# Two matmuls in place of three for each weight block: both parts of the activations side by side under the high weights, and the halves of a PSUM bank added behind

## The chip, the core and the metric

One core of one Trainium2 chip runs the whole program. The metric is the device time of the program in microseconds (us). TensorE (PE) multiplies, VectorE (DVE), ScalarE (ACT) and GpSimd (POOL) do everything elementwise, and SyncE (SP) issues the transfers of the weights. In the views, PEld is the weight load of a matmul, which overlaps the matmuls.

## The reference, cut to what matters

A trunk of two decoder layers over 256 tokens with 1024 channels, all in float32. Layer 0 mixes tokens with a short gated convolution, layer 1 with dilated windowed attention (8 heads in each of 3 groups, 128 channels a head, rotary on 32 of them). After each mixer comes a squared-ReLU MLP of 4096 channels and a gated per-layer input; a last rmsnorm ends it.

```python
def rmsnorm(x, g): return x * lax.rsqrt(jnp.mean(x * x, axis=-1, keepdims=True) + RMS_EPS) * g

def short_conv_mixer(h, w_in, w_conv, w_out):
    gate_b, gate_c, xin = jnp.split(h @ w_in, 3, axis=-1)
    y = gate_b * causal_depthwise_conv(gate_c * xin, w_conv)
    return y @ w_out

def squared_relu_mlp(h, w_up, w_down):
    return jnp.square(jax.nn.relu(h @ w_up)) @ w_down
```

The attention's three groups are weighed by the softmax of their log-sums of exponentials, so that one softmax over all keys of the three groups gives the same. The per-layer input is `sigmoid(rmsnorm(x) @ w_gate) * (p @ w_proj)`, added to x.

## The kernel before

**Products.** Every operand of a large product is held as two float32r parts, high and low, so that value = high + low, and a product is the sum of three: high weights by high activations, high weights by low activations, low weights by high activations. Activations lie with channels on partitions and the 256 tokens along a row. A *block* is one 128x128 piece of weights; in most stages ("w" blocks, channels by tokens) the weights are the stationary side, and `block()` issues three matmuls of 256 columns each (L804) that add into one half of an accumulator. An accumulator is one bank of PSUM, 128 partitions by 2 halves of 256, for two neighbouring blocks of columns ("a pair of columns"). There are 1808 such blocks. In the "t" blocks (the attention's v, the last gate and projection) the activations are stationary, and the three matmuls have 384 or 512 columns of weights.

**Weights.** They come in slabs of up to 8 blocks (512 KB) by one transfer each (L767), 273 in all, into RAW_BUFS buffers. `split_to` splits each slab: ACT copies it to the high part `whi` (L777), DVE subtracts to get the low part `wlo` (L269, in the helper `sub`, which every low part goes through). `weights` asks for the slab that stands LOOK = 5 ahead of the one in use, so that the splits stand among the other work of ACT and DVE in the order of the plan.

**Order.** `make_plan` writes PE's work as a list; the steps in it ("do") add what the other engines do. The Tile scheduler orders each engine's instructions by their place in the plan, with the steps named in URGENT and the small chain of a norm moved ahead by HURRY = 250 places. Each engine then works through its own list in order, and waits where an operand isn't there.

**Stages.** In order of time: the projection of layer 0 (`acc_p`), the conv's products C, X, B for four pairs of columns, each followed by `conv`; the mixer's output (`acc_o`, `mix_out`); up (`acc_u`, 16 pairs, `up_out` behind each); down (`acc_d`), all four pairs side by side for 24 of the 32 rows of blocks, then pair by pair; the gate (`acc_g`, `gate_out`), with the projection multiplied in; then heads 0 to 7: q and k of three groups (`acc_qk`, `qk_out`: times cosr L1037, two rotary pieces L1040, added on POOL L1046), v (`v_out`), and among the next head's products the scores, the turn (transposes `tp`, L1090) and the values (`o`); then w_o, up, down and the last gate with the final norm.

**Norms.** `h_ready` (L836, L837) makes the two parts `xh`, `xl` of h times the gain, and `squares` (L847, L849, L851) adds up the squares of a token on POOL. The 1/rms joins later: `stat` (ssq, L872 to L905) makes it a diagonal, `spread` (L913, L915) turns that into a row on every partition, and the row is multiplied in behind the product (L980, L991, L1011, L1022). In the conv stage `spread` stands in the middle of the first B.

Of the kernel before, what the change touches and what calls it, by code (L numbers as in the profile page):

```python
# [34 lines left out]
RAW_BUFS, SPLIT_BUFS, ACT_BUFS = 6, 7, 45  # L35

# Rows of a head: the rotary halves lie 32 partitions apart.
# [27 lines left out]
def mlp_plan(layer):  # L65
# [11 lines left out]
    nf = FF // P  # L77
# [32 lines left out]
def last_plan():  # L110
    """The second layer's gate, projection and the final norm, by tokens."""
# [27 lines left out]
def make_plan():  # L139
    plan = [("do", "begin")]  # L140
    plan += proj_plan()
    for c in range(NP):
        for s, what in ((1, "C"), (2, "X"), (0, "B")):
            for k in range(NK):
                for i in (0, 1):
                    plan.append(("w", "sc_in", k, s * NK + 2 * c + i, (what, c), i, "x0"))
                if (c, s, k) == (0, 0, 4):
                    plan.append(("do", "spread", 0))
            if (c, s) == (0, 1):
                plan.append(("do", "stat", 0))  # L150
        plan.append(("do", "conv", c))
    for k in range(4):
        for j in range(NP):
            for i in (0, 1):
                plan.append(("w", "sc_out", k, 2 * j + i, ("o", j), i, "y"))
    for j in range(NP):
        for k in range(4, NK):
            for i in (0, 1):
                plan.append(("w", "sc_out", k, 2 * j + i, ("o", j), i, "y"))
        plan.append(("do", "mix_out", 0, j))  # L160
# [17 lines left out]
    plan += v(0, (0,)) + [("do", "spread", 3)]  # L178
    plan += [("do", "qk_out", 0, g) for g in range(GROUPS)] + v(0, range(1, NK)) + [("do", "v_out", 0)]
    for h in range(1, HEADS):  # L180
        plan += qk(h, 0, range(NK)) + [("do", "qk_out", h, 0)]
        plan += qk(h, 1, range(NK)) + [("do", "scores", h - 1)] + [("do", "qk_out", h, 1)]
        plan += qk(h, 2, range(NK)) + [("do", "turn", h - 1)] + [("do", "qk_out", h, 2)]
        plan += v(h, range(4)) + [("do", "values", h - 1)] + v(h, range(4, NK)) + [("do", "v_out", h)]

    def wo(j, ks):
        return [("w", "w_o", k, 2 * j + i, ("o", j), i, "y") for k in ks for i in (0, 1)]

    last = HEADS - 1
    plan += [x for k in (0, 1) for j in range(NP) for x in wo(j, (k,))]  # L190
    plan.append(("do", "scores", last))
    plan += [x for k in (2, 3) for j in range(NP) for x in wo(j, (k,))]
    plan.append(("do", "turn", last))
    plan += wo(0, (4, 5, 6)) + wo(1, (4,)) + [("do", "values", last)]
    for j in range(1, NP):
        plan += wo(j, (5, 6) if j == 1 else (4, 5, 6)) + wo(j - 1, (7,)) + [("do", "mix_out", 1, j - 1)]
    plan += wo(NP - 1, (7,)) + [("do", "mix_out", 1, NP - 1)]
# [8 lines left out]
def columns(key, col):  # L206
    """The columns of a weight matrix that one block of the plan takes, in order."""
# [10 lines left out]
def make_slabs(plan):  # L218
    """Runs of weight blocks that are loaded together: [[(key, k, col, width)]]."""
# [16 lines left out]
def tile_trunk(ctx: ExitStack, tc: tile.TileContext, plan, slabs, ap, out):  # L236
# [16 lines left out]

    def bank(name):
# [28 lines left out]
    for op in plan:  # L283
        if op[0] != "do":
            key = (op[4], op[5])
# [45 lines left out]
    def block(kind, key, k, col, name, half, operand, m=0, cuts=1):  # L331
        if name not in opened:
            acc[name] = bank("acc_" + "_".join(map(str, name)))
        left[name, half] -= 1
        whi, wlo = weights((key, k, col))
        x = [t[:, k % 2, :] for t in state[operand][k // 2]]
        if kind == "w":
            dst = acc[name][:, half, :]
            pairs = ((whi, x[0]), (whi, x[1]), (wlo, x[0]))
        else:  # L340
# [3 lines left out]
            xhi, xlo = (t[:, half * P : (half + 1) * P] for t in x)  # L344
            pairs = ((xhi, whi), (xhi, wlo), (xlo, whi))
        for n, (a, b) in enumerate(pairs):
            nc.tensor.matmul(
                dst,
# [3 lines left out]
                stop=n == 2 and left[name, half] == 0,  # L352
# [4 lines left out]
    def close(name):  # L357
        opened.discard(name)
        # Names are used again in the second layer.
        return acc.pop(name)  # L360

# [1 line left out]
    def split_into(kind, j, src, cuts=1):  # L363
        if kind in ("p0", "p1"):
            hi, lo = held("ph", f"{kind}h", 1, F32R), held("pl", f"{kind}l", 1, F32R)
        else:
            hi, lo = act(f"{kind}h{j}", F32R), act(f"{kind}l{j}", F32R)
# [4 lines left out]
        state[kind][j] = (hi, lo)  # L372

    def h_ready(n, j):
        """h[j] holds norm n's input."""
        hi, lo = act(f"xh{n}_{j}", F32R), act(f"xl{n}_{j}", F32R)
# [4 lines left out]
        state[f"x{n}"][j] = (hi, lo)  # L381
        squares(n, j)

    def squares(n, j):
        """The squares' sum over the channels that a partition holds."""
        sq = act(f"sq{n}_{j}")
        if j == NP - 1 and n in (2, 3, 5):
            nc.scalar.activation(sq, h[j], AF.Square)
        else:
            nc.gpsimd.tensor_tensor(sq, h[j], h[j], ALU.mult)  # L390
        tot = act(f"tot{n}_{j}")
        nc.gpsimd.tensor_tensor(tot[:, 0, :], sq[:, 0, :], sq[:, 1, :], ALU.add)
        if j:
            nc.gpsimd.tensor_tensor(tot[:, 1, :], tot[:, 0, :], cur["sq"], ALU.add)
# [7 lines left out]
    def newton(v, name):  # L402
        """v ** -0.5"""
# [7 lines left out]
    def stat(n):  # L411
        """1 / rms of a token, on the token's partition: column 2 b for half b."""
# [21 lines left out]
    def stat_rows(n):  # L434
        """1 / rms ** 2 of each token, on each partition."""
# [14 lines left out]
    def spread(n):  # L450
        """A column's values, on each partition."""
# [7 lines left out]
        if n == 3:  # L459
            # Rows without a rotary half have angle 0.  # L460
# [4 lines left out]
    def begin():  # L465
# [3 lines left out]
        # The array's clock is low until it has worked for a while: products of ones until the weights are here.  # L469
# [48 lines left out]
    def conv(c):  # L518
        pc, px, pb = close(("C", c)), close(("X", c)), close(("B", c))
        cx = spool.tile([P, 2, S + 2], F32, tag="cx", name=f"cx{c}")  # L520
        nc.gpsimd.memset(cx[:, :, 0:2], 0.0)
        t = act(f"ct{c}")
        nc.vector.tensor_tensor(t, pc, both(rows[0, 2]), ALU.mult)
        nc.vector.tensor_tensor(cx[:, :, 2:], t, px, ALU.mult)
# [8 lines left out]
        b = act(f"cb{c}")  # L533
        nc.vector.tensor_tensor(b, pb, both(rows[0]), ALU.mult)
        nc.vector.tensor_tensor(b, b, z, ALU.mult)
        split_into("y", c, b)

    def mix_out(layer, j):
        nc.vector.tensor_tensor(h[j], close(("o", j)), h[j], ALU.add)
        h_ready(3 * layer + 1, j)  # L540

    def up_out(j):
        p = close(("u", j))
        r = act(f"r{j}")
        nc.scalar.activation(r, p, AF.Relu)
        hi, lo = act(f"uh{j}", F32R), act(f"ul{j}", F32R)
# [745 lines left out]
```

## Time and profile before

| | |
|---|---|
| three timed runs | 813.25, 813.15, 810.01 us; median 813.15 us |
| the profiled execution: span from its first to its last instruction | 809.0 us |
| its own time around the span | not given; the runs above lie 1.0 to 4.2 us over the span |
| DVE, PE groups, ACT, POOL | 736, 6282, 538 and 110 records |
| HBM read | 139.10 MB, 173 GB/s over the span |

The span is the profiled execution's own time as far as the page gives it. Each group of instructions is named by line, engine and operation, with output and inputs by the program's names. "Idle before" is the time that an engine stood still just before an instruction, and the name behind the arrow is what ended it. The DMA engines are busy for 55.3% of the span with the weights:

```profile
q1 hardware_dynamic: 41616, 140.17, 55.3%
```

Stages of the trace: the first product at 4.47 us, C at 13.52, the mixer's output at 87.23, up at 110.27, down at 202.66, gate at 294.83, q and k of head 0 at 319.70, head 1 at 348.87, w_o at 558.96, the second up at 586.06, down at 679.19, the last gate at 771.35; the last product ends near 800.4.

### The profile page before, as it was taken

What the parts mean: (1) busy time and instruction counts of PE and PEld (TensorE: products, weight loads), DVE (VectorE), ACT (ScalarE), POOL (GpSimd) and SP (SyncE); (2) the same over time, 40 slices, a digit from 0 to 9 for tenths busy, and PEclk for the clock granted to TensorE, in tenths of its full rate; (3) what the DMA queues carried; (4) which work ended last, traced back from release to release, by engine and by line L of the source; (5) the groups of instructions that cost most, each with busy time, mean ns of one, the idle gap of its engine ahead of it and who ended that gap; (6) DMA issues with size and microseconds to landing.
All of it is one profiled execution on the core that took longest, in us unless ns stands there. A gap on an engine that the chain in (4) does not pass through costs nothing.

```text
span 809.0 us, 15204 instructions
## 1 busy us (share of the span) xinstructions
PE 789.9 (98%) x6282; PEld 782.5 (97%) x6282; DVE 578.5 (71%) x736; ACT 401.1 (50%) x538; POOL 131.7 (16%) x110
## 2 busy tenths in 40 slices
PE   7999999999999999899999999999999999999996
PEld 7999999999999999898999999999999999999985
DVE  7986697686444588898868877877697666444855
ACT  7544456565433455545445445545565555333543
POOL 6100060000000154331121111211240000000331
PEclk9999999999999999999999999999999999999999
DMA  8876646656666653645455555455455555565511
GB/s 274 282 240 200 183 150 199 201 162 203 182 183 184 183 173 116 196 163 162 155 164 161 154 174 159 137 187 182 146 178 187 183 183 182 183 182 182 170 40 52
DMA packets 41684, 141.13 MB, mean 174 GB/s; under 512 B 4752, under 2 KB 5136, under 8 KB 41616
## 3 DMA queue, kind: packets, MB, share of 16 engines
q1 hardware_dynamic: 41616, 140.17, 55.3%
q8 instruction: 49, 0.80, 0.4%
q14 instruction: 19, 0.16, 0.1%
HBM read 139.10 MB, written 1.05 MB: 173 GB/s over the span
## 4 chain that ended last, share of the span: by engine, by line
PE 55%; DVE 2%; POOL 0%; issue 0%; POOLq 0%; DVEq 0%; ACT 0%; ACTq 0%
PE acc_qk L804 14%; PE acc_d L804 11%; PE acc_u L804 11%; PE acc_v L804 8%; PE acc_o L804 3%; PE acc_g L804 3%; PE tp L1090 1%; PE o L1111 1%; PE sc L1072 1%; DVE wlo L269 1%; PE o L1105 1%; PE sc L1069 1%; PE acc_p L804 1%; DVE rot L1040 0%; PE rows L1141 0%
## 5 line engine op out<-in xcount | busy, mean ns | idle before, releaser
L269 DVE TENSOR_TENSOR wlo<-raw,whi 128x1024 fp32r<-128x1024 f32 (+3 forms) x273 | 341.1, 1257 | 167.7 <-ACT whi L777 166.6
L777 ACT ACTIVATE whi<-raw 128x1024 fp32r<-128x1024 f32 (+3 forms) x273 | 277.0, 1017 | 295.0 <-PE acc_d L804 103.2
L804 PE MATMUL acc_u<-xl,whi 128*128 128x256 f32 x512 | 145.2, 284 | 0.3 <-DVE xl L837 0.3
L804 PE MATMUL acc_d<-uh,wlo 128*128 128x256 f32 x512 | 145.0, 283 | 0.0
L804 PE MATMUL acc_d<-uh,whi 128*128 128x256 f32 x512 | 145.0, 283 | 0.0
L804 PE MATMUL acc_d<-ul,whi 128*128 128x256 f32 x512 | 145.0, 283 | 0.0
L804 PE MATMUL acc_u<-xh,whi 128*128 128x256 f32 x512 | 145.0, 283 | 0.0
L804 PE MATMUL acc_u<-xh,wlo 128*128 128x256 f32 x512 | 145.0, 283 | 0.0
L804 PE MATMUL acc_qk<-xh,whi 128*128 128x256 f32 x384 | 109.3, 285 | 0.0
L804 PE MATMUL acc_qk<-xh,wlo 128*128 128x256 f32 x384 | 108.6, 283 | 0.0
L804 PE MATMUL acc_qk<-xl,whi 128*128 128x256 f32 x384 | 108.6, 283 | 0.0
L804 PEld LDWEIGHTS acc_u<-xl,whi 128*128 128x128 f32 x512 | 97.0, 189 | 0.6 <-DVE xl L837 0.5
L804 PEld LDWEIGHTS acc_u<-xh,whi 128*128 128x128 f32 x512 | 97.0, 189 | 0.0
L804 PEld LDWEIGHTS acc_u<-xh,wlo 128*128 128x128 f32 x512 | 97.0, 189 | 0.0
L804 PEld LDWEIGHTS acc_d<-uh,wlo 128*128 128x128 f32 x512 | 96.6, 189 | 0.0
L804 PEld LDWEIGHTS acc_d<-ul,whi 128*128 128x128 f32 x512 | 96.6, 189 | 0.0
L804 PEld LDWEIGHTS acc_d<-uh,whi 128*128 128x128 f32 x512 | 96.6, 189 | 0.0
L804 PEld LDWEIGHTS acc_qk<-xl,whi 128*128 128x128 f32 x384 | 73.5, 191 | 0.0
L804 PEld LDWEIGHTS acc_qk<-xh,wlo 128*128 128x128 f32 x384 | 73.5, 191 | 0.0
L804 PEld LDWEIGHTS acc_qk<-xh,whi 128*128 128x128 f32 x384 | 73.5, 191 | 0.0
L1046 POOL TENSOR_TENSOR qk<-qk,rot 48x512 f32<-48x512 f32 x24 | 44.6, 1858 | 172.8 <-DVE rot L1040 172.8
L847 POOL TENSOR_TENSOR sq<-h 128x512 f32<-128x512 f32 x11 | 18.3, 1667 | 225.9 <-DVE h L1012 166.8
(196 smaller groups left out, 1427.8 us busy)
## 6 DMA issues: line engine op xcount, KB each, us to landing
raw<-in_w SPq DMA_DIRECT2D x232, 512.0 KB, 3.6
raw<-in_w SPq DMA_DIRECT2D x32, 384.0 KB, 3.1
raw<-in_w SPq DMA_DIRECT2D x7, 256.0 KB, 6.0
h<-in_xT SPq DMA_DIRECT2D x4, 256.0 KB, 6.5
out<-ht SPq DMA_DIRECT2D x4, 256.0 KB, 2.0
pt<-in_pT SPq DMA_DIRECT2D x2, 256.0 KB, 4.2
mask<-in_mask SPq DMA_DIRECT2D x2, 256.0 KB, 4.2
gain<-in_gain SPq DMA_DIRECT2D x2, 256.0 KB, 4.2
```

The lines of the kernel that those rows point to most:

```text
L269: nc.vector.tensor_tensor(out, a, f32(b), ALU.subtract)
L777: nc.scalar.activation(hi[:, :width], t[:, :width], AF.Copy)
L804: nc.tensor.matmul(dst, a, b, start=n == 0 and name not in opened, stop=n == 2 and left[name, half] == 0, skip_group_check=True,)
L847: nc.gpsimd.tensor_tensor(sq, h[j], h[j], ALU.mult)
L1046: nc.gpsimd.tensor_tensor(t[:48], t[:48], r[:48], ALU.add)
L1069: nc.tensor.matmul(ps[:, :S], q[:, 0, own], k[:, 1, :], start=n == 0, stop=n == 2)
L1072: nc.tensor.matmul(ps[:, (g + 1) * P : (g + 2) * P], t[:, 0, own], t[:, 1, own], start=True, stop=True)
L1090: nc.tensor.transpose(ps[n // 2][:, n % 2, b * P : (b + 1) * P], sm[:, n * P : (n + 1) * P], ident)
L1105: nc.tensor.matmul(ps[:, 0, :], a, b[:, kb, :], start=kb == 0 and n == 0, stop=False, skip_group_check=True)
L1111: nc.tensor.matmul(ps[:, 0, b * P : (b + 1) * P], v12[:, b, g * P : (g + 1) * P], t[:, g, b * P : (b + 1) * P], start=False, stop=g == 1, ...
```

## The change

**Pairs.** The two parts of an activation lie side by side in one tile (`pair`, 128 x 2 parts x 2 x 256). A "w" block is two matmuls: low weights by the high part (256 columns) into the first half of a bank, and high weights by both parts (512 columns) over the whole bank. So each block of columns has a bank of its own (`acc_u_8_0`, `acc_u_8_1` where one `acc_u_8` was), and its value is the sum of the two halves.

**Sums.** What reads an accumulator adds the halves first. `sums` does it by an ACT copy of the second half and a DVE add of the first, for each of the two blocks (up, down, projection, gate, q and k, C, X, B); `add_banks` does it by two DVE adds for each block (the mixers' outputs).

**Moves.** `qk_out`'s product with cosr goes from DVE to POOL, and the rotary pieces read SBUF where they read PSUM. The conv's two products with the rows of 1/rms go from DVE to POOL. The squares go from POOL to ACT (all of them) and their sums from POOL to DVE. `up_out` takes maximum and square in one DVE instruction, ACT makes a copy in place of ReLU and square.

**Plan.** Down goes pair by pair over all 32 rows of blocks (with two banks for a pair, four pairs side by side would fill all eight banks). The mixers' outputs go by two pairs. In head 0 the sums of q and k come ahead of two rows of v's blocks, and `spread` behind them.

**Buffers.** RAW_BUFS 6 to 5, SPLIT_BUFS 7 to 6, the general ones 45 to 13 and 20 pairs. The order of the transfers stays. The comments and a first, unused copy of the inner functions are deleted, so that the line numbers fall.

```diff
-RAW_BUFS, SPLIT_BUFS, ACT_BUFS = 6, 7, 45
+RAW_BUFS, SPLIT_BUFS, ACT_BUFS, PAIR_BUFS = 5, 6, 13, 20
...
-    for k in range(nf - 8):
-        for j in range(NP):
-            for i in (0, 1):
-                plan.append(("w", down, k, 2 * j + i, ("d", j), i, "u"))
     for j in range(NP):
-        for k in range(nf - 8, nf):
+        for k in range(FF // P):
...
+    plan += [("do", "add_up", ("qk", 0, g)) for g in range(GROUPS)]
+    plan += v(0, (0, 1)) + [("do", "spread", 3)]
+    plan += [("do", "qk_out", 0, g) for g in range(GROUPS)] + v(0, range(2, NK)) + [("do", "v_out", 0)]
...
         if kind == "w":
-            dst = acc[name][:, half, :]
-            pairs = ((whi, x[0]), (whi, x[1]), (wlo, x[0]))
+            dst = acc[name]
+            products = ((dst[:, 0, :], wlo, x[0][:, k % 2, :]), (flat(dst), whi, flat(x[2][:, k % 2, :, :])))
...
+    def sums(name, t):
+        for i in (0, 1):
+            p = close((*name, i))
+            nc.scalar.activation(t[:, i, :], p[:, 1, :], AF.Copy)
+            nc.vector.tensor_tensor(t[:, i, :], p[:, 0, :], t[:, i, :], ALU.add)
+        return t
...
-        if j == NP - 1 and n in (2, 3, 5):
-            nc.scalar.activation(sq, h[j], AF.Square)
-        else:
-            nc.gpsimd.tensor_tensor(sq, h[j], h[j], ALU.mult)
+        nc.scalar.activation(sq, h[j], AF.Square)
         tot = act(f"tot{n}_{j}")
-        nc.gpsimd.tensor_tensor(tot[:, 0, :], sq[:, 0, :], sq[:, 1, :], ALU.add)
+        nc.vector.tensor_tensor(tot[:, 0, :], sq[:, 0, :], sq[:, 1, :], ALU.add)
...
-        nc.vector.tensor_tensor(t, pc, both(rows[0, 2]), ALU.mult)
-        nc.vector.tensor_tensor(cx[:, :, 2:], t, px, ALU.mult)
+        nc.gpsimd.tensor_tensor(pc, pc, both(rows[0, 2]), ALU.mult)
+        nc.gpsimd.tensor_tensor(pb, pb, both(rows[0]), ALU.mult)
+        nc.vector.tensor_tensor(cx[:, :, 2:], pc, px, ALU.mult)
...
+    def add_banks(j, name):
+        for i in (0, 1):
+            p = close((*name, i))
+            for part in (0, 1):
+                nc.vector.tensor_tensor(h[j][:, i, :], p[:, part, :], h[j][:, i, :], ALU.add)
...
-        nc.scalar.activation(r, p, AF.Relu)
-        nc.scalar.activation(hi, r, AF.Square)
-        nc.vector.tensor_tensor(r, r, r, ALU.mult)
+        r = sums(("u", j), act(f"r{j}"))
+        nc.vector.scalar_tensor_tensor(r, r, 0.0, r, ALU.max, ALU.mult)
+        nc.scalar.activation(hi, r, AF.Copy)
         sub(lo, r, hi)
...
     def qk_out(head, g):
-        p = close(("qk", head, g))
-        nc.vector.tensor_tensor(t, p, both(cosr), ALU.mult)
+        p, t = cur["qk", head, g]
+        nc.gpsimd.tensor_tensor(t, p, both(cosr), ALU.mult)
```

On PE, in the middle of the first up, before the change (a row of blocks for the two blocks of columns of pair 8; the name at the left is the accumulator, then the activations' part and the weights' part):

```order
L804 MATMUL acc_u_8_1989<-xh1_0_1300,whi55_1818 128x256
L804 MATMUL acc_u_8_1989<-xl1_0_1301,whi55_1818 128x256
L804 MATMUL acc_u_8_1989<-xh1_0_1300,wlo55_1819 128x256
L804 MATMUL acc_u_8_1989<-xh1_0_1300,whi55_1818 128x256
L804 MATMUL acc_u_8_1989<-xl1_0_1301,whi55_1818 128x256
L804 MATMUL acc_u_8_1989<-xh1_0_1300,wlo55_1819 128x256
```

The same two blocks with the change:

```order
L356 MATMUL acc_u_8_0_1694<-x1_0_1094,wlo55_1556 128x256
L356 MATMUL acc_u_8_0_1694<-x1_0_1094,whi55_1555 128x512
L356 MATMUL acc_u_8_1_1703<-x1_0_1094,wlo55_1556 128x256
L356 MATMUL acc_u_8_1_1703<-x1_0_1094,whi55_1555 128x512
```

Six matmuls of 256 columns became two of 256 and two of 512, and the product with the low weights is now the first of a block.

On DVE near the start, before (the splits of slabs 9 to 13 are `wlo9` to `wlo13`; `v_0` is the first step of layer 0's first norm, `diag_0_1` and `diag_0_2` its last):

```order
L269 TENSOR_TENSOR wlo9_301<-raw9_226,whi9_300 128x1024
L882 TENSOR_SCALAR v_0_355<-ssq0_352 128x4
L269 TENSOR_TENSOR wlo10_319<-raw10_232,whi10_318 128x1024
L863 TENSOR_TENSOR n1_0_358<-n0_0_357 128x4
L269 TENSOR_TENSOR wlo11_337<-raw11_253,whi11_336 128x1024
```

With the change:

```order
L376 TENSOR_TENSOR prj3_261<-acc_p_3_0_245,prj3_261 128x256
L376 TENSOR_TENSOR prj3_261<-acc_p_3_1_254,prj3_261 128x256
L276 TENSOR_TENSOR wlo9_291<-raw9_225,whi9_290 128x1024
L276 TENSOR_TENSOR wlo10_305<-raw10_246,whi10_304 128x1024
L276 TENSOR_TENSOR wlo11_319<-raw11_267,whi11_318 128x1024
L276 TENSOR_TENSOR wlo12_363<-raw12_282,whi12_362 128x1024
L276 TENSOR_TENSOR wlo13_369<-raw13_288,whi13_368 128x1024
L444 TENSOR_SCALAR v_0_338<-ssq0_335 128x4
```

The eight adds of the projection (the last two are shown) and four more splits of slabs now stand ahead of the norm's first step.

On DVE in the gate, before (`gs2` is the gate of pair 2, `hr2` the new h, `xl3_2` the low part for the next norm):

```order
L1022 TENSOR_TENSOR gs2_3812<-acc_g_2_3751,row_2_3702 128x512
L269 TENSOR_TENSOR wlo116_3917<-raw116_3681,whi116_3916 128x1024
L1024 TENSOR_TENSOR gs2_3812<-gs2_3812,prj2_250 128x512
L1030 TENSOR_TENSOR hr2_3816<-h2_85,gs2_3812 128x256 x2
L269 TENSOR_TENSOR wlo117_3949<-raw117_3752,whi117_3948 128x768
L837 SCALAR_TENSOR_TENSOR xl3_2_3820<-hr2_3816,gains_73,xh3_2_3819 128x256 x2
```

With the change:

```order
L376 TENSOR_TENSOR gs2_3134<-acc_g_2_0_3088,gs2_3134 128x256
L376 TENSOR_TENSOR gs2_3134<-acc_g_2_1_3097,gs2_3134 128x256
L276 TENSOR_TENSOR wlo117_3256<-raw117_3112,whi117_3255 128x768
L585 TENSOR_TENSOR gs2_3134<-gs2_3134,row_2_3037 128x512
L276 TENSOR_TENSOR wlo118_3279<-raw118_3156,whi118_3278 128x768
L587 TENSOR_TENSOR gs2_3134<-gs2_3134,prj2_240 128x512
L593 TENSOR_TENSOR hr2_3142<-h2_85,gs2_3134 128x256 x2
L276 TENSOR_TENSOR wlo119_3301<-raw119_3179,whi119_3300 128x768
L402 SCALAR_TENSOR_TENSOR x3_2_3145<-hr2_3142,gains_73,x3_2_3145 128x256 x2
L411 TENSOR_TENSOR tot3_2_3152<-sq3_2_3150 128x256
```

Two adds stand ahead of the product with the row and a sum of squares behind the low part; three splits of 768 columns stand in between where one of 1024 and one of 768 did.

More of the change, by code (lines that the diff above doesn't have):

```diff
@@ L351, in block @@
                 start=n == 0 and name not in opened,
-                stop=n == 2 and left[name, half] == 0,
+                stop=n == len(products) - 1 and left[name] == 0,
                 skip_group_check=True,
@@ L907, in spread @@
-    def spread(n):
-        for key in ((n, 2), n):
-            if key in diags:
-                ps, t = bank(f"spread_{n}"), diags.pop(key)
-                for part in (0, 1):
-                    nc.tensor.matmul(ps[:, 0, :], ones_r, t[:, part, :], start=part == 0, stop=part == 1)
-                rows[key] = spool.tile([P, S], F32, tag="row", bufs=3, name=f"row_{n}")
-                nc.scalar.activation(rows[key], ps[:, 0, :], AF.Copy)
-        if n == 3:
-            nc.vector.tensor_tensor(cosr, cosr, rows[n], ALU.mult)
-            nc.vector.tensor_tensor(sinr, sinr, rows[n], ALU.mult)
```

515 lines of the change are left out of this document (62 added, 453 removed).

## The prediction, on record before the changed kernel ran

> **What bounds the kernel now.** I read the shares of the engines first, then the waits of PE, then the chain that ended last, and then each stage by itself.
>
> ```profile
> span 809.0 us, 15204 instructions
> PE 789.9 (98%) x6282; PEld 782.5 (97%) x6282; DVE 578.5 (71%) x736; ACT 401.1 (50%) x538; POOL 131.7 (16%) x110
> PE ssq L872 <- POOL tot L851: 3.5, 2, 2.6
> PE acc_C L804 <- DVE wlo L269: 2.9, 3, 1.5
> PE tp L1090 <- DVE st L1080: 1.9, 1, 1.9
> PE acc_u L804 <- DVE xl L837: 0.3, 1, 0.3
> ```
>
> PE works for 98% of the span. Its few waits on others are the sums of squares ahead of a norm's products (3.5 us), the weights' low parts at the start (2.9), the first turn in the attention (1.9) and one at the second up (0.3). So the time falls with PE's work as long as the others keep up, and the question is how far PE's work falls and where DVE, at 71%, becomes the later one.
>
> ```profile
> 430.47 4.17 PE acc_v L804 x24
> 610.23 69.12 PE acc_u L804 x576
> 679.35 92.16 PE acc_d L804 x768
> 790.82 2.04 PE acc_g L804 x9
> 800.39 0.03 issue
> ```
>
> In the chain PE runs without a gap over long stretches, and these rows price a product: 92.16 us / 768 = 120.0 ns for 256 columns (69.12 / 576 gives the same), 4.17 / 24 = 173.7 ns for 384, 2.04 / 9 = 226.7 ns for 512. These lie on a line: 53.4 ns for each 128 columns, and 13.3 ns for each product whatever its length. The last product ends at 800.4; the 8.6 us behind it are a tail which the change does not touch.
>
> ```profile
> 23.33:87.23 63.90, 63.90 (x534) 63.90 (x534) 52.08 (x74) 31.39 (x38) 2.16 (x3) 1.00 0.74 235
> 110.27:202.66 92.39, 92.39 (x772) 92.39 (x771) 71.53 (x87) 54.56 (x70) 7.23 (x7) 1.00 0.57 185
> 202.66:294.83 92.17, 92.17 (x771) 92.17 (x769) 50.15 (x46) 37.79 (x40) 9.65 (x8) 1.00 0.62 182
> 294.83:348.87 54.04, 50.53 (x399) 50.12 (x398) 44.70 (x66) 27.64 (x38) 21.53 (x18) 1.00 0.49 158
> 348.87:558.96 210.09, 208.24 (x1597) 207.71 (x1597) 171.88 (x247) 103.49 (x157) 42.29 (x23) 1.00 0.52 162
> 430.10:459.78 29.68, 29.68 (x231) 29.68 (x230) 23.60 (x35) 14.51 (x23) 5.71 (x3) 1.00 0.55 161
> ```
>
> By stage (length, then busy PE, weight load, DVE, ACT, POOL, then granted clock, DMA share, GB/s): conv, first up, first down, gate to the first v, the seven heads, and one head in the middle of them. DVE has 11.8 us free in the conv stage, 20.9 in an up, 42 in a down, 9.3 from the gate on, and 6.1 in a head. DMA is busy for 0.49 to 0.74 and the bytes stay, so I leave it out.
>
> **The change, part by part.** *The products.* A block was three products of 256 columns, 360.0 ns; it becomes one of 256 and one of 512, 120.0 + 226.7 = 346.7 ns. The columns are as many as before; one fixed cost of 13.3 ns falls away. There are 1808 such blocks: **-24.1 us**. The 512-column product of before has its activations as the stationary side; here the weights are, but a product between others of its kind is paced the same in the 256-column rows whatever it multiplies. The bounds are nothing (0) and 24.1.
>
> The Trainium skill has a rule here that speaks against this change (TensorE: Matmul & The Clock Gate, Back-to-back issue gap): an isolated warm product takes N/2.4 + 2.5 ns, so the fixed part would be 2.5 ns and the saving an estimated 1808 x 2.5 = 4.5 us. The trace does not agree: by that rule 256 columns take 109.2 ns where the row has 120.0.
>
> *The sums.* What they cost on DVE and ACT has its price in rows of like form.
>
> ```profile
> L269 DVE TENSOR_TENSOR wlo<-raw,whi 128x1024 fp32r<-128x1024 f32 x232 | 301.6, 1307 | 153.2 <-ACT whi L777 152.6
> L1037 DVE TENSOR_TENSOR qk<-acc_qk,cosr 128x512 f32<-128x512 f32 x24 | 16.4, 684 | 6.7 <-PE acc_qk L804 6.7
> L1159 DVE TENSOR_TENSOR gs<-gs,acc_p 128x256 f32<-128x256 f32 x2 | 0.8, 418 | 0.4 <-ACT gs L1150 0.4
> L1122 ACT ACTIVATE oh<-o 128x256 fp32r<-128x256 f32 x8 | 3.1, 384 | 4.1 <-PE o L1111 4.1
> L269 DVE TENSOR_TENSOR qkl<-qk,qkh 128x512 fp32r<-128x512 f32 x8 | 5.5, 690 | 11.1 <-ACT qkh L827 11.1
> L1046 POOL TENSOR_TENSOR qk<-qk,rot 48x512 f32<-48x512 f32 x24 | 44.6, 1858 | 172.8 <-DVE rot L1040 172.8
> L847 POOL TENSOR_TENSOR sq<-h 128x512 f32<-128x512 f32 x11 | 18.3, 1667 | 225.9 <-DVE h L1012 166.8
> ```
>
> An add of 128x256 from PSUM is 0.418 us on DVE and a copy 0.384 on ACT: 0.84 and 0.77 for a pair of columns. In an up that is 16 x 0.84 = 13.4 us more on DVE, for 20.9 us free less 256 x 13.3 ns = 3.4 us of saving, so 17.5: it fits, and ACT (54.56 of 92.39) has room. A down adds 3.3 against 42. In both I take nothing, under the cover of slabs split five ahead; without that cover an up loses as much as DVE lacks. In the conv stage DVE gets 24 adds (10.0), gives 8 products to POOL (8 x 0.684 = 5.5) and ends near 52.08 + 4.5 = 56.6 of 63.90 - 2.6 = 61.3: it fits too, with 4.7 us to spare.
>
> *The start, +5.0.* There the order matters.
>
> ```profile
> 19.18 1.83 DVE L837 SCALAR_TENSOR_TENSOR xl<-h,gains,xh 128x256 fp32r<-128x256 f32 x2
> 23.51 0.16 DVE L882 TENSOR_SCALAR v<-ssq 128x4 f32<-128x4 f32 x1 [0.76 <-PE ssq L872]
> 30.89 0.61 DVE L905 SCALAR_TENSOR_TENSOR diag<-ident,r,diag 128x128 fp32r<-128x128 f32 x2
> 32.76 0.64 PE L913 MATMUL spread<-diag,ones_r 128*128 128x256 f32 x4
> ```
>
> DVE takes the norm's first step at 23.51 and ends the diagonals at 31.5, 1.3 us before PE's spread at 32.76. With the change eight adds (3.3) and four more splits (four by 1.22 = 4.9) stand ahead of that first step, and three of these splits (3.7) no longer stand behind it; two sums of squares (0.8) come over from POOL, less 0.3 that POOL no longer slows. The diagonals end 5.0 later, at 36.5, while PE would be there at 33.2: it loses 3.3, with the rest of B's products queued behind. PE also loses 1.7 at the first C and X, where the products wait for the same splits: the adds put 3.3 ahead of them, and two pairs of low parts without POOL's squares beside them give 1.6 back (the row at 19.18 took 1.83 where that at 332.12, below, took 0.95). The bounds are 0 (DVE is no longer slowed by POOL's squares, which doubled the row at 19.18, and that covers the adds) and 8.2 (all that is put ahead).
>
> *From the gate to the first v, +5.1.* This stage already ran behind.
>
> ```profile
> 314.94 0.68 DVE L1022 TENSOR_TENSOR gs<-acc_g,row 128x512 f32<-128x512 f32 x1
> 322.21 0.68 DVE L1022 TENSOR_TENSOR gs<-acc_g,row 128x512 f32<-128x512 f32 x1
> 322.81 1.21 DVE L269 TENSOR_TENSOR wlo<-raw,whi 128x1024 fp32r<-128x1024 f32 x1
> 324.66 1.16 DVE L1030 TENSOR_TENSOR hr<-h,gs 128x256 f32<-128x256 f32 x2
> 325.75 0.95 DVE L269 TENSOR_TENSOR wlo<-raw,whi 128x768 fp32r<-128x768 f32 x1
> 328.68 0.68 DVE L1022 TENSOR_TENSOR gs<-acc_g,row 128x512 f32<-128x512 f32 x1
> 332.12 0.95 DVE L837 SCALAR_TENSOR_TENSOR xl<-hr,gains,xh 128x256 fp32r<-128x256 f32 x2
> 335.43 0.61 PE ssq L872 x4
> ```
>
> DVE begins a pair every 7.3 and 6.5 us where PE needs 16 x 0.36 = 5.8, and the sums on POOL made PE wait 2.6 at 335.43. With the change pair 2 is, on DVE, adds 0.84, products 0.68 twice, h 1.16, low part 0.95 (no POOL beside it), sums 0.84 and three splits by 0.95: 8.0 us; pair 3 has one split, 6.1, and about 1 us of waits for ACT's copies and sigmoid. PE needs 16 x 0.347 = 5.55 for each: 15.1 - 11.1 = 4.0, and the sums of squares end about 1.1 later than these. So the norm of layer 1 and the first heads' products come 5.1 us late. Bounds: -2.6 (the wait for POOL's sums goes and nothing takes its place) and 8.6 (the splits of the other pairs are late as well).
>
> *The heads, +3.5.* DVE in a head: 23.60, less three products with cosr (2.05), plus six adds (2.5). POOL gets three products of 128x512 (1.67 each), and while POOL works DVE is slower:
>
> ```profile
> 305.10 2.41 DVE L269 TENSOR_TENSOR wlo<-raw,whi 128x1024 fp32r<-128x1024 f32 x2
> 434.83 3.45 DVE L269 TENSOR_TENSOR wlo<-raw,whi 128x1024 fp32r<-128x1024 f32 x2
> 434.94 2.25 POOL L1046 TENSOR_TENSOR qk<-qk,rot 48x512 f32<-48x512 f32 x1 [4.96 <-DVE rot L1040]
> 369.74 1.16 PE tp L1090 x8
> ```
>
> Two splits take 2.41 alone and 3.45 beside 2.25 us of POOL, 0.46 us for each us. Three products bring 3 x 1.67 x 0.46 = 2.3, so DVE comes to 26.4 of PE's 29.68 - 48 x 0.0133 = 29.04. It fits in the sum, but the slack falls from 6.1 to 2.7 and some of it is bound to places (waits for ACT's parts, for the scores). I take 0.3 in each of six heads, and 1.7 for the first, which had no lead before either: the chain of DVE ahead of the turn at 369.74 gets six adds and loses three products (+0.45) and has POOL beside it for another 2.7 us (+1.2). The bounds: 0, and 4.1 a head (rival D).
>
> *w_o and the second up, -0.3.* The wait for xl goes: POOL's squares no longer stand beside it.
>
> The sum: -24.1 + 5.0 + 5.1 + 3.5 - 0.3 = **-10.8 us**, a span of 798.2. The profiled execution is not timed by itself; its span lies 4.2 us under the median of 813.15, and I put the same behind the change: 802.
>
> **The rivals.** *B, all of the saving stays.* DVE's lead of five slabs covers the sums, and the waits stay what they were: -24.1, 789. For it: 29% of DVE is free. Against it: the stage from the gate on has PE waiting for DVE's side already.
>
> *C, nothing is left.* DVE's free time is bound to its places: a head then takes 30.7 (26.4 of work and 4.3 of the 6.1 idle), 7 x 1.65 = 11.6 in place of 3.5, and each of the conv's four pairs loses 0.7: -10.8 + 8.1 + 2.8 = 0.1, 813. For it: 11.1 us of DVE's idle time stand before one instruction that waits for ACT's part (the row of qkl). Against it: the scheduler puts splits into such places.
>
> *D, slower: POOL and DVE shut each other out in the heads.* If DVE stands for all the time that POOL multiplies, three products are 5.0 a head; and the six rotary pieces, which now read two operands in SBUF as the splits do, double from 0.68 (+4.1): 23.60 - 2.05 + 2.5 + 9.1 = 33.2 for PE's 29.04. Seven heads lose 28.8 in place of 3.5: -10.8 + 25.3 = +14.5, 828. It decides for slower from 31.1 a head. For it: the split beside POOL grew by half. Against it: 0.46 and not 1.
>
> The Trainium skill has this as a rule (SBUF — State Buffer, Who interferes with whom): a DVE instruction with two inputs in SBUF contends with a GpSimd instruction that reads SBUF, for a lock that blocks the other wholly. The trace agrees that they contend; the share of 0.46 is less than a full block.
>
> *E, the longer product saves next to nothing.* The second half of a bank, or the alternation of 256 and 512 columns, could cost what the third product did: 346.7 becomes 357.5, 4.5 us in all are saved and the 13.3 of the other terms stay: +8.8, 822. Against it: the straight line through three lengths. This would also be the result by the skill's fixed part above.
>
> **How the numbers follow.** Forecast 0.42, B 0.14, C 0.20, D 0.17, E 0.07. A measurement of this kernel can tell about 0.5%, 4.1 us, from no change. Faster by more: the forecast, B and a part of C, 0.62; within it 0.14 from C; slower D and E, 0.24. The range takes in B with a gain of some us at the gate (-26.7 with that term at its lower bound, 786.5), and goes up to E and the lower half of D, 823; beyond it lies about half of D and little else.
>
> **What would show it.** Long stretches of PE in down and up should show 173.4 ns for each product (346.7 a block): at 180 E holds. At the start the wait of PE's spread for the diagonals should be near 3 us, at the gate the waits of PE for x3 and the sums near 8.6 in all. A head should last 29.0 to 29.4; at 30.7 C holds and at 33 D, and the windows then show DVE busy for nearly all of it, with rot near 1.3 us. The forecast is wrong if PE waits in ups or downs for the splits.

## The result, and the profile after

The changed kernel takes 821.18 us (median of 4 runs, 820.0 to 822.05), the kernel before 812.31 us beside it. The ratio is 1.0116, with a 95% interval of 1.0091 to 1.0142: slower by 1.2%, where the forecast was 1.3% faster. The profiled execution took 820.0 us, 1.8 over its span of 818.2, and that span is 9.2 longer than the 809.0 of before.

From the page of the changed kernel, the head and the engines; then PE's waits (in all, times, longest); then two rows of its chain; then the windows of conv, first up, first down, gate to first v, seven heads, and one head:

```profile
span 818.2 us, 11902 instructions
PE 775.7 (95%) x4474; PEld 689.2 (84%) x4474; DVE 631.5 (77%) x938; ACT 441.3 (54%) x691; POOL 111.8 (14%) x79
```

```profile
PE tp L652 <- DVE st L642: 21.1, 7, 8.6
PE acc_C L356 <- DVE prj L376: 4.9, 1, 4.9
PE acc_qk L356 <- ACT x L401: 4.2, 3, 2.6
PE acc_qk L356 <- DVE gs L376: 1.6, 1, 1.6
```

```profile
625.33 66.56 PE acc_u L356 x384
...
691.90 88.75 PE acc_d L356 x512
```

```profile
25.33:86.91 61.58, 61.58 (x358) 54.36 (x358) 53.73 (x81) 33.97 (x57) 14.30 (x10) 1.00 0.63 206
109.10:198.08 88.98, 88.98 (x515) 78.49 (x514) 77.95 (x120) 56.13 (x85) 0.00 (x0) 1.00 0.59 195
198.08:286.83 88.75, 88.75 (x513) 78.25 (x512) 51.36 (x59) 41.06 (x51) 0.00 (x0) 1.00 0.58 191
286.83:343.81 56.98, 50.92 (x286) 43.93 (x284) 46.71 (x87) 33.96 (x56) 8.52 (x6) 1.00 0.49 151
343.81:576.45 232.64, 211.15 (x1261) 194.10 (x1261) 194.47 (x267) 114.55 (x199) 82.06 (x47) 0.96 0.46 145
405.27:436.69 31.42, 29.35 (x180) 26.94 (x181) 26.52 (x38) 16.11 (x29) 10.65 (x6) 1.00 0.48 150
```

Three things are to be seen. First, the products do what they were to do: 66.56 us / 384 and 88.75 / 512 are both 173.3 ns for the mean of a 256- and a 512-column product, 346.7 ns a block. Conv, up and down are shorter than before by what their blocks save (an up by 3.41, a down by 3.42, forecast 256 x 13.3 ns = 3.4), and PE waits for nobody in them. Second, PE has new waits, 21.1 us of them at the turns `tp`, seven times. Third, the heads take 232.64 us where 210.09 stood before, though DVE is busy for only 26.52 of 31.42 us in one of them.

The stages by PE's first instructions, in us:

| stage | before | after | difference | saving of its blocks | lost |
|---|---|---|---|---|---|
| start to first X | 23.33 | 25.33 | +2.00 | 0.43 | 2.4 |
| conv from X | 63.90 | 61.58 | -2.32 | 2.34 | 0 |
| mixer's output, up, down | 207.60 | 199.92 | -7.68 | 7.66 | 0 |
| gate to head 1 | 54.04 | 56.98 | +2.94 | 1.49 | 4.4 |
| seven heads | 210.09 | 232.64 | +22.55 | 4.47 | 27.0 |
| w_o and second up | 120.23 | 115.29 | -4.94 | 4.26 | -0.7 |
| second down | 92.16 | 88.74 | -3.42 | 3.41 | 0 |
| last gate to the end | 37.65 | 37.72 | +0.07 | 0 | 0.1 |

24.1 us were saved and 33.2 lost, 27.0 of them in the heads: 9.8 in the first, and 17.2 in the other six (the turn waits 2.08 in each, 12.5 in all; twice the clock falls behind it, at 1.6 each; and a head is about 0.3 longer than this wait accounts for, 31.42 less 29.04 less 2.08).

In one head, DVE and then POOL of the changed kernel, in time (start, length, line, operation, names, shapes, count, idle before), and PE's turn behind them:

```profile
422.90 2.51 DVE L602 TENSOR_TENSOR rot<-qk,sinr 16x512 f32<-16x512 f32 x2
...
428.24 0.69 DVE L276 TENSOR_TENSOR qk<-qk,qk 128x512 fp32r<-128x512 f32 x1 [1.84 <-ACT qk L392]
...
429.85 0.75 DVE L376 TENSOR_TENSOR qk<-acc_qk,qk 128x256 f32<-128x256 f32 x2
430.52 0.68 DVE L637 CUSTOM_DVE_ANT_0 sm<-sc,mask 128x512 f32<-128x512 f32 x1
...
431.24 1.28 DVE L602 TENSOR_TENSOR rot<-qk,sinr 16x512 f32<-16x512 f32 x1
...
434.19 0.95 DVE L276 TENSOR_TENSOR wlo<-raw,whi 128x768 fp32r<-128x768 f32 x1
435.05 1.49 DVE L643 TENSOR_SCALAR sm<-sm,st 128x512 f32<-128x512 f32 x1
```

```profile
422.88 1.30 POOL L599 TENSOR_TENSOR qk<-qk,cosr 128x512 f32<-128x512 f32 x1 [8.82 <-DVE qk L376]
425.55 1.99 POOL L608 TENSOR_TENSOR qk<-qk,rot 48x512 f32<-48x512 f32 x1 [1.38 <-DVE rot L602]
430.68 1.30 POOL L599 TENSOR_TENSOR qk<-qk,cosr 128x512 f32<-128x512 f32 x1 [3.14 <-DVE qk L376]
434.17 2.09 POOL L608 TENSOR_TENSOR qk<-qk,rot 48x512 f32<-48x512 f32 x1 [2.19 <-DVE rot L602]
```

```profile
436.69 1.16 PE L652 MATMUL tp<-ident,sm 128*128 128x128 f32 x8 [2.08 <-DVE st L642]
```

Two rotary pieces in the kernel before:

```profile
433.43 1.37 DVE L1040 TENSOR_TENSOR rot<-acc_qk,sinr 16x512 f32<-16x512 f32 x2
```

At 422.88 POOL starts the product with cosr, and the two rotary pieces beside it take 2.51 us where two took 1.37 before. POOL's add waits for them, ACT's split for the add, and DVE's low part (428.24) for ACT, with the softmax of the head before queued behind it. Then a third piece stands beside the next product (1.28 for 0.68). Last, the softmax's product `sm` stands beside POOL's add and takes 1.49 us (0.49 alone); before the change it had come ahead of that add. The turn follows at 436.69, 2.08 us after PE was ready for it.

### The profile page after: what moved, and what is told of

Read it like the earlier page. It is cut to its first block, busy times and chain, and to the rows that moved or that the text cites. A ratio compares the mean times of both kernels' runs of the same rounds, so it can differ in the third digit from the quotient of the medians.

```text
span 818.2 us, 11902 instructions
## 1 busy us (share of the span) xinstructions
PE 775.7 (95%) x4474; PEld 689.2 (84%) x4474; DVE 631.5 (77%) x938; ACT 441.3 (54%) x691; POOL 111.8 (14%) x79
## 4 chain that ended last, share of the span: by engine, by line
PE 43%; DVE 11%; issue 3%; POOL 2%; ACT 2%; POOLq 0%; DVEq 0%; ACTq 0%
PE acc_u L356 11%; PE acc_d L356 11%; PE acc_v L356 8%; PE acc_qk L356 5%; DVE rot L602 3%; PE acc_o L356 3%; PE acc_g L356 3%; DVE wlo L276 2%; POOL qk L608 2%; DVE qk L376 1%; PE tp L652 1%; DVE sm L643 1%; ACT whi L327 1%; DVE sm L637 1%; PE o L673 1%
## 5 line engine op out<-in xcount | busy, mean ns | idle before, releaser
L356 PE MATMUL acc_u<-x,whi 128*128 128x512 f32 x512 | 177.7, 391 | 0.0
L356 PE MATMUL acc_d<-u,whi 128*128 128x512 f32 x512 | 177.6, 391 | 0.0
L356 PE MATMUL acc_d<-u,wlo 128*128 128x256 f32 x512 | 143.4, 280 | 0.0
L356 PE MATMUL acc_u<-x,wlo 128*128 128x256 f32 x512 | 143.4, 280 | 0.0
L356 PE MATMUL acc_qk<-x,whi 128*128 128x512 f32 x384 | 133.6, 394 | 0.1
L356 PEld LDWEIGHTS acc_d<-u,whi 128*128 128x128 f32 x512 | 95.7, 187 | 21.0
L356 PEld LDWEIGHTS acc_u<-x,whi 128*128 128x128 f32 x512 | 95.7, 187 | 20.9
L356 PE MATMUL acc_qk<-x,wlo 128*128 128x256 f32 x384 | 106.5, 281 | 6.2 <-ACT x L401 4.2
L356 PEld LDWEIGHTS acc_d<-u,wlo 128*128 128x128 f32 x512 | 96.8, 189 | 0.0
L356 PEld LDWEIGHTS acc_u<-x,wlo 128*128 128x128 f32 x512 | 96.8, 189 | 0.0
```

The source lines that it names most:

```text
L356: nc.tensor.matmul(to, a, b, start=n == 0 and name not in opened, stop=n == len(products) - 1 and left[name] == 0, skip_group_check=True,)
```

## The experiments

Theories: **1**, POOL's products with cosr hold up DVE in the heads; **2**, the sums and copies do it by standing in DVE's and ACT's queues; **3**, fewer buffers for slabs starve the heads. Later two questions were added: whether the place of the softmax decides, and what the gate and the start lose to.

| run | time, us | ratio to before (95%) | seven heads | gate to head 1 |
|---|---|---|---|---|
| changed kernel | 821.18 | 1.0116 (1.0091 to 1.0142) | 232.64 | 56.98 |
| q and k in three products | 805.45 | 0.991 (0.9896 to 0.9925) | 216.14 | 57.14 |
| no product with cosr | 802.38, one run | - | 213.98 | 57.00 |
| cosr on DVE | 804.13 | 0.9914 (0.9881 to 0.9946) | 214.89 | 58.56 |
| projection in three | 820.34 | 1.0119 (1.0078 to 1.0159) | 232.78 | 56.91 |
| cosr on DVE, scores early | 796.24 | 0.9794 (0.977 to 0.9818) | 208.53 | 58.52 |
| the same, gate in three | 792.75 | 0.9746 (0.972 to 0.9771) | 209.98 | 51.50 |
| rotary pieces from PSUM | 798.82, one run | - | 210.19 | 57.13 |
| before, fewer buffers | 817.78, one run | - | 215.86 | 55.82 |
| scores early alone | 799.35 | 0.984 (0.9809 to 0.987) | 210.57 | 58.67 |
| gate and projection in three | 792.75 | 0.9761 (0.9718 to 0.9803) | 208.39 | 51.42 |

**q and k in three products.** The old form of a block for q and k alone, without their sums, and with head 0 planned as before the change:

```diff
+OLD_FORM = ("qkv",)
...
+        if key in OLD_FORM:
+            dst, (xh, xl) = acc[name][:, half, :], (t[:, k % 2, :] for t in x[:2])
+            products = ((dst, whi, xh), (dst, whi, xl), (dst, wlo, xh))
...
-        p, t = cur["qk", head, g]
-        nc.gpsimd.tensor_tensor(t, p, both(cosr), ALU.mult)
+        p, t = close(("qk", head, g)), act(f"qk{head}_{g}")
+        nc.vector.tensor_tensor(t, p, both(cosr), ALU.mult)
```

> Against the changed kernel: the 384 blocks of q and k are three products of 256 columns into one bank again, with the product by cosr on DVE from PSUM and without sums; all else stays. Theory 1 (POOL's products with cosr hold up DVE's work in the heads) and theory 2 (the sums stand in DVE's and ACT's queues ahead of the softmax): the seven heads fall from 232.6 us to 211 or 212, so the span from 818.2 to about 797 and the time to 799, faster than the kernel before. Theory 3 (fewer buffers for slabs, 5 and 6 in place of 6 and 7, starve the heads): the heads stay over 225 and the time over 812.

Faster than before by 0.9%, but the heads stay at 216.14 and not 211 or 212. So the change outside q and k is a gain on balance (the gate still takes 57.14 us). This run takes the sums and POOL's product away together, so it doesn't choose between theories 1 and 2; and something still costs 1 us a head (30.67 us from turn to turn, 29.68 before), which neither of them has.

**No product with cosr.** Left out: q and k times cosr; the rotary pieces are added into the sums.

```diff
-        p, t = cur["qk", head, g]
-        nc.gpsimd.tensor_tensor(t, p, both(cosr), ALU.mult)
+        p = t = cur["qk", head, g][0]
```

> The product of q and k with cosr is left out; the sums stay, and the rotary pieces are added into them on POOL. Theory 1: the rotary pieces fall from 1.16 to about 0.7 us each, the turns' wait of 2.08 us goes, a head is 29.0 to 29.4 and the first one under 36: span about 797. Theory 2: a wait of 1.4 us or more stays at each turn, a head is 30.5 or more, span about 811.

The group of the rotary pieces by line, in the changed kernel and then in this run:

```profile
L602 DVE TENSOR_TENSOR rot<-qk,sinr 16x512 f32<-16x512 f32 x48 | 55.6, 1159 | 1.7
```

```profile
L601 DVE TENSOR_TENSOR rot<-qk,sinr 16x512 f32<-16x512 f32 x48 | 33.7, 701 | 1.7
```

1.159 us becomes 0.701, with the same inputs in SBUF. The turns' wait falls from 2.08 to 0.38 us, a head to 29.72; the first still takes 4.78 of wait. DVE's instructions stand in the same order in both runs, so 1.7 of the 2.08 us are POOL's product: 1.1 through the two pieces of 422.90 and 0.6 through the third. Theory 1 holds for most; 0.7 a head stay, and a head of 29.0 to 29.4 did not come.

**The product with cosr on DVE.**

```diff
-        nc.gpsimd.tensor_tensor(t, p, both(cosr), ALU.mult)
+        nc.vector.tensor_tensor(t, p, both(cosr), ALU.mult)
```

> The product with cosr goes back to DVE, now from the sums in SBUF; the sums stay. Theory 1: DVE is busy for about 24.7 of a head in place of 26.5, the wait at the turn falls to 0.7 or less, a head to 30 or less, the time to about 807. Theory 2: with 0.69 us more ahead of the softmax in DVE's queue the wait grows to about 2.7, a head is 32, and the time 824.

One word takes 17 us off (821.18 to 804.13), though DVE gets more to do: the window of one head shows DVE at 26.65 us, not the 24.7 of theory 1's estimate, and yet the head is shorter.

```profile
431.08:460.94 29.86, 29.29 (x181) 26.95 (x181) 26.65 (x41) 16.33 (x29) 5.73 (x3) 1.00 0.50 160
```

So what counts is not how busy DVE is but whether the work ahead of the turn is held up. What remains is a wait of 0.57 us in the middle of each turn.

**The projection in three products**, four banks in place of eight and no add:

```diff
-        cur["prj", j] = sums(("p", j), act(f"prj{j}"))
+        t = cur["prj", j] = act(f"prj{j}")
+        nc.scalar.activation(t, close(("p", j)), AF.Copy)
```

> The projection of layer 0 (16 blocks) in three products of 256 columns, four banks in place of eight, with one ACT copy and no add. If the first C waits for a bank that the projection's adds give back (4.89 us of wait): C starts by 14.5 in place of 17.4, its products at half the clock go, X starts at about 23, and the time falls by 2.0 to 2.5 us. If C is held up by its own operands (the splits and the parts of x on DVE) in any case: X still starts near 25 and the time stays within 0.7.

Each reading was right in part. The first row is PE's first C in the changed kernel; then this run's first X:

```profile
17.37 0.55 PE L356 MATMUL acc_C<-x,wlo 128*128 128x256 f32 x1 [4.89 <-DVE prj L376]
```

```profile
22.27 0.55 PE L362 MATMUL acc_X<-x,wlo 128*128 128x256 f32 x1 [2.80 <-DVE n L432]
```

C starts at 12.73 and X at 22.27, so the bank was what C waited for. But then X waits 2.80 us for the split of its slab, which stands in DVE's queue behind the norm's first steps, the clock falls there in place of C (0.50 from 22.27 to 27.00), and the mixer's output starts 0.23 us earlier only. The wait has moved, and the time is the same within its interval.

**The scores ahead.** What is left at the turn is a question of place: in the run with cosr on DVE the split of a slab (1.98 us, beside POOL's add) stood between the last two products of the softmax. The scores' step now goes ahead with the urgent ones, so that PE makes the scores of head h-1 behind the first group of head h.

```diff
-URGENT = ("gate_out", "mix_out", "down_out", "begin")
+URGENT = ("scores", "gate_out", "mix_out", "down_out", "begin")
```

> The product with cosr on DVE as in the run before, and the scores' step among those moved ahead, so that PE makes the scores of head h-1 behind the first group of head h and not behind the second, and the softmax has 5.5 us more before the turn. If what is left of the wait at the turn is only the place of the softmax in DVE's queue: the waits of 0.57 us and of 0.27 in the second half of a turn go, a head is 29.0 to 29.2, the first head loses 1 to 2 us less, and the time is 797 to 800. If DVE is full in the heads (26.65 busy of 29.86): the wait comes back at another place (values, sums of q and k), a head stays at 29.6 or more, and the time at 803 or more.

PE's turn, 29.07 us behind the one before it and without a wait:

```profile
427.19 1.03 PE L652 MATMUL tp<-ident,sm 128*128 128x128 f32 x8
```

From turn to turn it is 29.07 and 29.09 us, where PE's own products need 29.04: no wait is left in the six heads, with all the sums in place. So what theory 2 had left was a matter of place. The time is 796.24 us, a little under the 797 to 800 expected.

**The gate in three products** beside that:

```diff
-        s = sums(("g", j), act(f"gs{j}"))
-        nc.vector.tensor_tensor(s, s, both(rows[2]), ALU.mult)
+        s = act(f"gs{j}")
+        nc.vector.tensor_tensor(s, close(("g", j)), both(rows[2]), ALU.mult)
```

> As the run with the scores ahead, and the gate's 64 blocks in three products of 256 columns with four banks in place of eight, without sums. By the theory that the gate's sums make q and k of head 0 late (a bank that waits 1.6 us for an add, the parts of x 1.4 and 2.6 us late): the stretch from the gate to the first v, 50.0 us with the cosr product on DVE, falls by 2.0 to 4.0 less the 0.85 that the products cost, and the time by 1 to 3 us against that run. If the splits of slabs hold DVE there in any case: no gain, 0 to 1 us slower.

The window from the first product of q and k to the first v, with the scores ahead and then with the gate in three products too:

```profile
311.20:337.24 26.04, 20.29 (x101) 16.52 (x100) 19.37 (x37) 13.35 (x27) 2.55 (x2) 0.93 0.45 144
```

```profile
312.07:330.76 18.69, 17.57 (x102) 15.13 (x101) 17.36 (x36) 11.43 (x21) 1.01 (x1) 1.00 0.58 195
```

The gain there is 7.4 us, more than expected: the waits of 1.64 for a bank and of 1.38 and 2.59 for x are gone (one of 1.11 for the sum of squares is new), and with them a fall of the granted clock (0.93 and 1.00). In the changed kernel the clock didn't fall in this stretch, which took 24.72, so that some 1.3 of the 7.4 are the clock of that one execution. The first head gives 1.45 back, and the time falls by 3.5, a little more than expected. The run takes the gate's sums and its four additional banks away together; which of the two counts more is not shown.

**The rotary pieces from PSUM**, with as many POOL products as in the changed kernel: q and k in the old form as in the first run, and

```diff
-        nc.vector.tensor_tensor(t, p, both(cosr), ALU.mult)
+        nc.scalar.activation(t, p, AF.Copy)
+        nc.gpsimd.tensor_tensor(t, t, both(cosr), ALU.mult)
```

> q and k in three products in one bank without sums, the rotary pieces read PSUM as before the change, ACT copies the bank to SBUF, and POOL multiplies by cosr there, as many POOL products as in the changed kernel. If a DVE instruction stands beside POOL only where both of its inputs lie in SBUF: the rotary pieces take 0.68 us on average though POOL works beside them. If POOL's product slows any DVE instruction beside it: they stay over 1.0 us.

Its pieces and POOL's products, by line:

```profile
L608 DVE TENSOR_TENSOR rot<-acc_qk,sinr 16x512 f32<-16x512 f32 x48 | 32.7, 681 | 3.4 <-POOL qk L614 2.1
...
L605 POOL TENSOR_TENSOR qk<-qk,cosr 128x512 f32<-128x512 f32 x24 | 35.3, 1473 | 119.7 <-ACT qk L604 115.4 <-DVE cosr L485 4.3
```

Two pieces beside a product, POOL first:

```profile
414.00 1.58 POOL L605 TENSOR_TENSOR qk<-qk,cosr 128x512 f32<-128x512 f32 x1 [11.25 <-ACT qk L604]
```

```profile
414.45 1.39 DVE L608 TENSOR_TENSOR rot<-acc_qk,sinr 16x512 f32<-16x512 f32 x2
```

The mean is 0.681 us, as before the change. 31 of the 48 pieces overlap one of the 24 products (1.47 us each) by 0.15 us or more, and none of these took over 0.683; in the changed kernel the 31 that overlap one took 1.39 on average. So POOL's product holds up the piece that has both inputs in SBUF, not the one with an input in PSUM.

**Before, with fewer buffers.**

```diff
-RAW_BUFS, SPLIT_BUFS, ACT_BUFS = 6, 7, 45
+RAW_BUFS, SPLIT_BUFS, ACT_BUFS = 5, 6, 45
```

> The kernel before with RAW_BUFS 5 and SPLIT_BUFS 6, nothing else. Theory 3 (fewer buffers for slabs cost the heads about 1 us each, as the 30.67 us of a head with q and k in three products suggests): a head goes from 29.68 to 30.3 or more and the time to 817 or more. If the buffers don't matter and the 30.67 come from where a split of a slab stands in the softmax: a head stays at 29.7 and the time within 1.5 us.

The number is theory 3's: a head goes to 30.67 us and the time to 817.78. DVE ahead of a turn, before and then in this run:

```profile
457.32 0.68 DVE L1040 TENSOR_TENSOR rot<-acc_qk,sinr 16x512 f32<-16x512 f32 x1
458.04 0.49 DVE L1081 TENSOR_SCALAR sm<-sm,st 128x512 f32<-128x512 f32 x1
458.44 2.31 DVE L269 TENSOR_TENSOR wlo<-raw,whi 128x1024 fp32r<-128x1024 f32 x1
```

```profile
460.22 0.49 DVE L1081 TENSOR_SCALAR sm<-sm,st 128x512 f32<-128x512 f32 x1
460.62 0.16 DVE L1080 RECIPROCAL st<-st 128x1 f32<-128x1 f32 x1
460.69 2.24 DVE L269 TENSOR_TENSOR wlo<-raw,whi 128x1024 fp32r<-128x1024 f32 x1
462.85 0.47 DVE L1081 TENSOR_SCALAR sm<-sm,st 128x512 f32<-128x512 f32 x1
```

But the way is not starvation: in the heads PE waits for no slab, only for the softmax at the turns (4.7 us in six waits). With fewer buffers the scheduler puts a split of a slab ahead of the softmax's last product, and the turn waits 0.77 us in its middle. The run with q and k in three products has the same 0.77 and the same 30.67; the one with the pieces from PSUM has the same few buffers and 29.68. So the buffers cost by the order that they lead to.

**The scores ahead alone**, with POOL's products left where the change put them:

> The changed kernel with the scores' step moved ahead alone; the product with cosr stays on POOL. If the delay by POOL only matters because the softmax stands behind it with no slack: with 5.5 us more ahead of the turn the six later heads are 29.0 to 29.4, the stretch of seven heads 212 or less, and the time 800 or less. If DVE beside POOL has no slack left in a head (26.5 busy of 29.04, plus what it waits): heads stay at 30 or more and the time over 808.

The six heads take 29.07 to 29.09 us each, and the time is 799.35. In the profiled execution, of 805.46 us, the first up and down are 2% longer than in the changed kernel, so only its heads are read here:

```profile
432.00:461.10 29.10, 29.10 (x182) 27.04 (x181) 27.65 (x39) 16.21 (x28) 11.11 (x6) 1.00 0.52 164
```

The rotary pieces still take 1.21 us on average, DVE is busy for 27.65 of 29.10, and PE waits for nothing in these heads: there POOL's hold on DVE costs nothing once the softmax has slack. It isn't free everywhere. In the first head PE waits 2.36 us for POOL's add ahead of the scores, a wait that the run with cosr on DVE does not have; that head takes 36.08 us for 34.05 there, and the medians lie 3.1 us apart.

**Gate and projection in three products**, cosr on DVE, scores ahead:

> The best so far (cosr on DVE, scores ahead, gate in three products) with the projection's 16 blocks in three products as well. By the run with the projection alone in three products the wait of C for its bank (4.97 us) and the half clock behind it go, and X waits for the split of its slab behind the norm's first steps: the mixer's output starts 0.2 to 1.2 us earlier, the time falls by as much, within 0.3% of the best. If the start then follows the bank alone: 2.5 us earlier.

The same median, 792.75, with runs from 788.47 to 795.8: nothing that could be told from the run without the projection's edit. The profiled execution, the fastest of the four, starts its mixer's output 2.7 us earlier, as by the second reading; the clock fell less behind its X (0.62 in the first 4.55 us) than in the run with the projection alone (0.50). The best version of the study is thus either of the two, 2.4 to 2.5% faster than before.

## Why the prediction was wrong

The time of 821 lies inside the range, but the sign is the other one. The range's upper end stood for E and the lower half of D, and of these D came, in its mechanism; that its 28.8 us for the heads lie near the measured 27.0 is in part luck, as will be seen.

*The products, -24.1.* Right: 346.7 ns a block, and conv, up and down lost nothing, as forecast. Rival E falls. So does the fixed part of 2.5 ns of the Trainium skill (TensorE: Matmul & The Clock Gate, Back-to-back issue gap) for these products, where the rows give 13.3.

*The start, +5.0.* It lost 2.4, by another way. The forecast 3.3 at the spread did not come: the diagonals end at 32.75, 1.25 us later than before and not 5.0, and PE reaches the spread at 34.44 only. It was late already, by a wait of 4.89 us, because the first C needs a bank which the projection's eight accumulators hold until DVE's adds are done. The eight banks were not counted at this place. Before, PE had lost 2.9 in C itself, so that the net is small.

*Gate to the first v, +5.1.* It lost 4.4: near in size, and the run with the gate in three products shows that the gate's sums, with the banks that they take, are the cause. PE's waits there are 5.8 us where 8.6 were forecast, and the one of 1.6 for a bank had not been foreseen.

*The heads, +3.5.* This is the step that failed: 27.0. DVE's busy time was forecast well (26.4, measured 26.52), though the pieces alone got 2.7 us a head longer (six times 1.159 less 0.701) where 2.3 had been put down for everything. Wrong was what was done with it. The step spread POOL's hold over all of DVE's work, at 0.46 us for each us, and set the sum against the length of a head. But the hold falls on the rotary pieces, which had just been moved to two operands in SBUF, at 1.14 us for a product of 1.30, and those of the first two groups stand in DVE's queue ahead of the turn, which has no slack (0.38 us of wait even without the products): 1.1 by way of POOL's add and ACT's split, 0.6 by one more piece, and the 0.38 make up the wait of 2.08. The row of 0.46 came from two splits beside the add of 48 partitions, not from a piece beside a product of 128. *Rival D* named this mechanism and a threshold of 31.1 us a head; measured were 31.42 and, with the slower clock, 33.0. Its picture of DVE as full was wrong: 4.9 us of a head were idle, and its sum of 28.8, which had every head at 33.2, is met only with 9.8 us in the first head and two falls of the clock.

The rule of the Trainium skill given with D (SBUF — State Buffer, Who interferes with whom) was the better guide: 0.701 us without the products, 1.159 with them, 0.681 with an input in PSUM agree with its lock for two inputs in SBUF.

*The clock* was left out of the sum. It fell to half after the wait of 4.89 us (4.2 us at half the clock, some 2 us lost) and after three turns (about 1.6 each). The granted clock stands third from the end:

```profile
17.37:21.60 4.23, 4.23 (x14) 3.65 (x15) 4.23 (x9) 3.03 (x4) 0.00 (x0) 0.50 0.94 351
...
437.60:441.20 3.60, 3.60 (x16) 3.60 (x15) 3.57 (x6) 1.64 (x4) 0.38 (x1) 0.57 0.58 191
```

*w_o and the second up, -0.3:* -0.7 came; what the other 0.4 are was not traced. *The time around the span* was put at 4.2 us and is 1.8 in the profiled execution.

Not settled: how the 9.8 us lost in the first head divide. Its wait was 8.59 with the products on POOL, 4.78 without them, 3.36 with cosr on DVE and 2.19 with q and k in three products. So 3.8 us of the wait go with the products; that the sums and the late gate share the rest is a guess, since no run takes either away alone.

## What to carry to other kernels

Where work is moved between engines, don't add up an engine's busy time and compare it with a stage; follow the one chain that ends at the waiting engine, and price each instruction on it with what will run beside it on the other engines. Before an engine is relieved, see whether a step placed earlier makes room: here moving the scores ahead took 22 us off, taking the product off POOL 17. And count the banks where accumulators double.

## What the hardware showed that was not expected

A pause of PE of 2.08 us, once in 31 us, was enough to halve the granted clock for about 4 us behind it, but in two of six equal heads only; in the run with the projection in three products, whose heads are the same but for their start, it was again two of six, one of them another one. The Trainium skill (TensorE: Matmul & The Clock Gate, HAM oscillation — how this bites in real kernels) puts the limit at an idle gap of about 3.4 us; here the shorter pause did it at times.

A DVE product with a single tensor in SBUF (`sm` by a scalar a row) took 1.49 us beside POOL's add and 0.49 alone, so it is held up as well, where the add began first; in the run with cosr on DVE one that began 0.11 us ahead of the add took 0.48. The rotary piece with one input in SBUF and one in PSUM was not held up (0.68 beside a product that had begun first).
